# Low parts of a trunk's projection weights formed by accumulating DMA instead of VectorE

## The chip, the cores and the metric

One core of a Trainium2 chip runs the kernel. The metric is the device time of one execution in microseconds, the median of three runs. TensorE (PE) multiplies, VectorE (DVE), ScalarE (ACT) and GpSimd (POOL) do the element-wise work, SyncE (SP) issues most transfers, and 16 DMA engines move the bytes. A matmul here takes operands in a reduced 32-bit format (fp32r). Where full float32 accuracy is wanted, each operand is split into a high part (the value rounded to fp32r) and a low part (the value less its high part), and three matmuls are added up.

## The reference, cut to what matters

```
for layer in range(2):
    xn = rms_norm(h)                                   # (512, 1024)
    proj = xn @ w_in[layer]                            # w_in: 1024 x 4608, nine groups of 512 columns
    rq, rk, rv, rg, hq, hf_fwd, hf_bwd, hi, hg = split(proj)
    r_out = retention(rq, rk, rv) * silu(rg)           # 4 heads
    h_out = hgrn2(hq, hf_fwd, hf_bwd, hi) * silu(hg)   # 4 heads, both directions
    h = h + concat(r_out, h_out) @ w_out[layer]        # w_out: 1024 x 1024
    h = h + expert_choice_ffn(rms_norm(h))             # 16 SwiGLU experts, 64 tokens each
return rms_norm(h)
```

## The kernel before

A layer has two stages. The **mixer** makes the nine projections one after the other (proj 0 to proj 8; the order of the column groups is `GROUPS`), does the HGRN2 and retention work beside them, and ends with the output product with w_out. The **experts** stream their weights from HBM through the same slots.

Memory is cut into 22 slots of 8 KB per partition. `slot` takes the one that has been free longest, `put` gives one back; a new owner waits for the last readers of the old one. The weights w_in come as 18 tiles a layer of 1024 KB (512 rows by 512 columns, `raw`), two tiles per projection.

`split` makes the parts of half a tile (128 x 1024 elements) at a time: ScalarE copies it to the high part (line 436), and VectorE, in a few places GpSimd, subtracts to get the low part (line 438). `proj` is a generator: it goes through four quarters q of the contraction, 24 matmuls each (line 465), in threes: high weights with high input, low weights with high input, high weights with low input. So the second matmul of a quarter already needs the low part. At the start of quarter q, the split for quarter q + 1 is written. After every six matmuls it yields.

`lead` runs a projection and, at each yield, takes steps of a side generator until a budget is used up. That sets the order of the instructions on every engine; each engine then runs its own list strictly in that order and waits on semaphores. Beside proj 3 to proj 6 runs `hgrn`: per pair of heads a start (lines 568 to 583, whose results line 591 multiplies) and six levels, in which VectorE and GpSimd update factors (lines 551, 556, 561), ScalarE copies keys (line 531) and TensorE multiplies them (line 604). Beside proj 7 run the rest of it, the retention, and the first half of `wout_split`; beside proj 8 the norms and the second half. `wout_split` does for w_out what `split` does for w_in (lines 806 and 807). Evacuations of a projection's four PSUM banks (lines 477 and 478 for proj 1 and 2, line 503 for proj 7, lines 789 to 796 for proj 8) are ScalarE and VectorE work. `pump` loads tiles ahead, in the mixer at most two.

Of the kernel before, what the change touches and what calls it, by code (L numbers as in the profile page):

```python
# [10 lines left out]
F32R = mybir.dt.float32r  # L11
BF = mybir.dt.bfloat16
U8 = mybir.dt.uint8
AF = mybir.ActivationFunctionType
OP = mybir.AluOpType
# [50 lines left out]
class Kernel:  # L66
# [55 lines left out]
    def plan(self):  # L122
        a = self.a
        for l in range(self.depth):
            for g in self.GROUPS:
                for j in range(2):
                    n = 2 if g == self.GROUPS[0] and j == 0 else 1
                    self.wq.append((("in", l, g, j),
# [203 lines left out]
    def begin(self, l):  # L332

        self.mix_layer, self.nsplit, self.parts, self.wo = l, 0, {}, {}
        self.turned = {}

    def turn_in(self, ks, banks):
# [81 lines left out]
    COSTS = (1.2, 1.3, 0.65, 1.9)  # L419
    BUDGET = (1.0, 1.2, 1.0, 0.9, 2.2, 1.3)  # L420
    GROUPS = (4, 5, 6, 7, 0, 1, 2, 3, 8)

    def split(self, upto):


        nc = self.nc
        while self.nsplit <= min(upto, 4 * len(self.GROUPS) - 1):
            i = self.nsplit
            self.nsplit += 1
            g, j, jj = self.GROUPS[i // 4], i % 4 // 2, i % 2  # L430
            if jj == 0:
                self.raw = self.take(("in", self.mix_layer, g, j))
            part = self.slot([2, 2, 512], F32R)
            wh, low = part[:, 0], part[:, 1]
            src = self.raw.rearrange("p a k c -> p (a k) c")[:, 2 * jj:2 * jj + 2]
            nc.scalar.activation(wh, src, AF.Copy)  # L436
            e = nc.gpsimd if self.GROUPS[i // 4] in (7, 2) and i % 2 or i == 0 else nc.vector
            e.tensor_tensor(low, src, wh, op=OP.subtract)  # L438
            self.parts[i] = part
            if jj:  # L440
                self.put(self.raw)

    def proj(self, n, natural, evacuate):


        nc = self.nc
        pg = [self.pj() for _ in range(4)]
        for q in range(4):
            self.split(4 * n + q + 1)
            part = self.parts.pop(4 * n + q)  # L450
            wh, low = part[:, 0], part[:, 1]

            order = [(c, k2) for k2 in range(2) for c in range(4)] if n == 0 and q < 3 else \
                [(c, k2) for c in range(4) for k2 in range(2)]
            for i, (c, k2) in enumerate(order):
                cs = slice(c * P, (c + 1) * P)
                k = 2 * q + k2
                H, L = wh[:, k2], low[:, k2]
                xh, xl = self.xH[k // 4][:, k % 4], self.xL[k // 4][:, k % 4]
                if natural:  # L460
                    ops = ((xh[:, cs], H), (xh[:, cs], L), (xl[:, cs], H))
                else:
                    ops = ((H[:, cs], xh), (L[:, cs], xh), (H[:, cs], xl))
                for m, (lhsT, rhs) in enumerate(ops):
                    nc.tensor.matmul(pg[c], lhsT=lhsT, rhs=rhs, start=(k == 0 and m == 0), stop=(k == ND - 1 and m == 2))  # L465
                if k == ND - 1:
                    evacuate(c, pg[c])
                if i == 7:
                    self.put(part)
                if i % 2:  # L470
                    yield

# [325 lines left out]
    def wout_split(self, l):  # L798
        nc = self.nc
        for f in range(2):  # L800
            for j in range(2):
                raw = self.take(("out", l, f, j))
                wh, low = self.slot([4, 512], F32R), self.slot([4, 512], F32R)
                for i in range(2):
                    part = slice(2 * i, 2 * i + 2)
                    nc.scalar.activation(wh[:, part], raw[:, part], AF.Copy)
                    (nc.vector if i or f > j else nc.gpsimd).tensor_tensor(low[:, part], raw[:, part], wh[:, part], op=OP.subtract)  # L807
                    yield 0.6
                self.put(raw)
                self.wo[f, j] = (wh, low)  # L810

    def lead(self, gen, side=None, budget=0.0):


        credit = 0.0
        for _ in gen:
            self.pump(ahead=2, kinds=("in", "out"))
            credit += budget
            while side is not None and credit > 0.0:
                cost = next(side, None)  # L820
                if cost is None:
                    break
                credit -= cost

    def mixer(self, l):
        nc = self.nc
        self.norm1(l)
        self.rope = self.tmp4([2, S])
        nc.sync.dma_start(self.rope, self.a["rope"])
        if l == 0:  # L830
            self.const_rows()
        self.lead(self.proj(0, False, self.silu_q))
        if l == 0:
            self.more_consts()
        self.F = [self.slot([2, 2, S]) for _ in range(2)]
        self.K = [self.slot([2, 2, S]) for _ in range(2)]
        for n, d in ((1, 1), (2, 0)):
            self.lead(self.proj(n, False, lambda c, ps: self.forget(l, d, c, ps)))
        self.oh = None
        self.hsq = self.t2.tile([P, S], F32, name=f"hsq{l}", tag="tn", bufs=1)  # L840
        hg = self.hgrn()
        B = self.BUDGET
        self.lead(self.proj(3, True, lambda c, ps: self.copy_out("v2", c, ps)), hg, B[0])
        self.left = ()
        for n, nm in ((4, "rq"), (5, "rk")):
            self.lead(self.proj(n, False, lambda c, ps: self.rotate(nm, c, ps)), hg, B[n - 3])
        self.add_late()
        self.lead(self.proj(6, True, lambda c, ps: self.copy_out("rv", c, ps)), hg, B[3])
        wo = self.wout_split(l)

        def eighth():
            yield from hg
            yield from self.retention()
            for _ in range(4):
                yield next(wo)
        side = eighth()
        self.lead(self.proj(7, False, lambda c, ps: self.gate_out("rg", 4 * l, c, ps)), side, B[4])
        for _ in side:
            pass

        def ninth():
            yield from self.norms()
            yield from wo
        side = ninth()
        self.lead(self.proj(8, False, lambda c, ps: self.mix_out(8 + 4 * l, c, ps)), side, B[5])
        for _ in side:
            pass
        self.put(*self.xH, *self.xL, self.oh)
        self.load_h(self.hd if l > 0 else self.xv)
        self.xe = self.slot([ND, 2 * P])  # L870
        self.pump()
        self.output(l)
# [497 lines left out]
```

## Time and profile before

| | us |
|---|---|
| median of three runs | 1640.59 (1637.1 to 1641.18) |
| the profiled execution | 1637.67 |
| its span in the trace | 1635.8 |
| TensorE busy in the span | 1531.0 |
| VectorE busy | 664.4 |
| ScalarE busy | 474.9 |
| GpSimd busy | 229.3 |

The span is cut into stages in which different engines are the limit, so the shares of the whole say little about the mixer alone. Layer 0's mixer lies from 0 to 370 us (first expert matmul, line 1145), its experts from there to some 820 us, layer 1's mixer from there to 1179 us, and its experts take the rest. The profiled execution is 1.87 us longer than its span and 2.9 us shorter than the median.

### The profile page before, as it was taken

The numbers are of one execution on the slowest core, as the hardware profiler recorded it, in microseconds if no ns is written. First come the engines' busy times: TensorE is split into PE (matmuls) and PEld (weight loads), VectorE is DVE, ScalarE is ACT, GpSimd is POOL, SyncE is SP. The second block draws the span as 40 slices with busy tenths as digits, with TensorE's granted clock in tenths as the row PEclk, the third lists the DMA queues.
The fourth block names the chain that finished last, engine by engine and source line by source line (L and its number), as shares of the span: only waits on it lengthen the run. The fifth ranks groups of instructions, "written<-read, shape, count | busy, mean of one in ns | idle before, by whom it ended". The sixth has DMA issues, their size and how long they took to land. (4 is left out here: it accounts for less than half of the span.)

```text
span 1635.8 us, 19932 instructions
## 1 busy us (share of the span) xinstructions
PE 1531.0 (94%) x7970; PEld 954.9 (58%) x7970; DVE 664.4 (41%) x1107; ACT 474.9 (29%) x889; POOL 229.3 (14%) x201
## 2 busy tenths in 40 slices
PE   7989899969999999999999899999699999999986
PEld 6878798754354534533478787977444445444333
DVE  5378945561121312212254889464511122212113
ACT  4334444542221200200343434455322202112003
POOL 3042542100000000011021344430000000000201
PEclk9999999989999999999999999999799999999998
DMA  7211132577999999999941211317699999999997
GB/s 262 75 53 52 52 124 78 211 303 301 427 425 426 427 426 427 426 427 427 400 176 51 78 41 64 123 52 258 273 385 427 420 427 426 427 427 426 426 426 275
DMA packets 94605, 464.53 MB, mean 284 GB/s; under 512 B 7904, under 2 KB 16288, under 8 KB 48432
## 3 DMA queue, kind: packets, MB, share of 16 engines
q1 hardware_dynamic: 93040, 458.35, 69.0%
q0 software_dynamic: 1472, 4.90, 0.8%
q8 instruction: 63, 1.03, 0.2%
q14 instruction: 30, 0.25, 0.0%
HBM read 459.03 MB, written 4.19 MB: 283 GB/s over the span
## 5 line engine op out<-in xcount | busy, mean ns | idle before, releaser
L1145 PE MATMUL pj<-s,s 128*64 128x512 f32 x2048 | 478.8, 599 | 19.2 <-DMA s<-in_w_up_dram 13.9
L465 PE MATMUL pj<-s,s 128*128 128x512 f32 x1728 | 426.7, 401 | 12.9 <-DVE s L438 8.6
L465 PEld LDWEIGHTS pj<-s,s 128*128 128x128 f32 x1728 | 324.2, 192 | 82.7 <-DVE s L438 11.6
L1145 PEld LDWEIGHTS pj<-s,s 128*64 128x64 f32 x2048 | 173.3, 137 | 279.6 <-issue 203.3
L1265 PE MATMUL pb<-s,t 128*64 128x512 f32 x896 | 197.8, 594 | 5.4 <-ACT t L1183 2.7
L1272 POOL TENSOR_TENSOR s<-s,s 128x1024 f32<-128x1024 f32 x8 | 18.7, 2362 | 872.1 <-DVE s L1205 823.5
L1265 PEld LDWEIGHTS pb<-s,t 128*64 128x64 f32 x896 | 66.0, 137 | 126.8 <-issue 110.8
L1193 DVE SCALAR_TENSOR_TENSOR t<-pb,sm,t 128x512 fp32r<-128x512 f32 (+1 forms) x34 | 24.5, 719 | 242.5 <-ACT t L1192 241.0
L1205 DVE TENSOR_TENSOR s<-s,pb 128x512 f32<-128x512 f32 (+1 forms) x112 | 67.3, 661 | 130.0 <-PE pb L1200 130.0
L909 PE MATMUL pj<-s,s 128*128 128x512 f32 x384 | 96.6, 400 | 3.4 <-DVE s L796 2.9
L438 DVE TENSOR_TENSOR s<-s,s 128x1024 fp32r<-128x1024 f32 x62 | 84.3, 1383 | 37.8 <-ACT s L436 37.6
L1110 DVE COPY sm<-pb 128x2 f32<-128x2 f32 x16 | 2.5, 159 | 210.9 <-PE pb L1107 210.9
L909 PEld LDWEIGHTS pj<-s,s 128*128 128x128 f32 x384 | 69.3, 189 | 20.7 <-DVE s L796 4.6
L1192 ACT ACTIVATE t<-pb,sm 128x512 fp32r<-128x512 f32 (+1 forms) x34 | 22.5, 662 | 195.4 <-PE pb L1265 183.2
L1088 PEld LDWEIGHTS pb<-t,t 128*128 128x128 f32 x512 | 64.9, 199 | 17.3 <-issue 15.0
L1121 ACT ACTIVATE t<-pb 128x512 fp32r<-128x512 f32 x16 | 9.6, 601 | 221.0 <-PE pb L1119 221.0
L436 ACT ACTIVATE s<-s 128x1024 fp32r<-128x1024 f32 x72 | 73.4, 1048 | 0.0
L1088 PE MATMUL pb<-t,t 128*128 128x256 f32 x512 | 69.8, 293 | 3.2 <-DVE t L1072 2.4
L1200 PE MATMUL pb<-t,t 128*128 128x512 f32 (+1 forms) x256 | 66.7, 401 | 0.1
L556 DVE TENSOR_TENSOR s<-s,s 128x512 f32<-128x512 f32 x56 | 59.3, 1059 | 13.4 <-PE pb L604 13.4
L1200 PEld LDWEIGHTS pb<-t,t 128*128 128x128 f32 x256 | 44.7, 188 | 33.0 <-issue 19.4
L531 ACT ACTIVATE s<-s 128x256 f32<-128x256 f32 x96 | 35.3, 415 | 93.8 <-DVE s L551 93.5
(237 smaller groups left out, 1541.2 us busy)
## 6 DMA issues: line engine op xcount, KB each, us to landing
s<-in_w_gate_dram SPq DMA_DIRECT2D x124, 1024.0 KB, 19.5
s<-in_w_up_dram SPq DMA_DIRECT2D x124, 1024.0 KB, 19.6
s<-in_w_down_dram SPq DMA_DIRECT2D x112, 1024.0 KB, 19.6
s<-in_w_in_dram SPq DMA_DIRECT2D x34, 1024.0 KB, 5.9
s<-in_w_down_dram SPq DMA_DIRECT2D x32, 512.0 KB, 9.4
s<-in_w_out_dram SPq DMA_DIRECT2D x8, 1024.0 KB, 4.8
s<-in_x_dram SPq DMA_DIRECT2D x8, 512.0 KB
s<-in_w_gate_dram SPq DMA_DIRECT2D x8, 512.0 KB, 5.6
```

What stands on the lines that cost most here:

```text
L436: nc.scalar.activation(wh, src, AF.Copy)
L438: e.tensor_tensor(low, src, wh, op=OP.subtract)
L465: nc.tensor.matmul(pg[c], lhsT=lhsT, rhs=rhs, start=(k == 0 and m == 0), stop=(k == ND - 1 and m == 2))
L531: self.nc.scalar.activation(kv[:, :, e], src, AF.Copy)
L556: v.tensor_tensor(qv, qv, tq, op=OP.mult)
L909: nc.tensor.matmul(po, lhsT=x, rhs=w, start=(k == 0 and i == 0), stop=(k == ND - 1 and i == 2))
L1088: nc.tensor.matmul(pt[:, i], lhsT=x[:, tt, k % 2::2], rhs=oh[:, tt], start=(tt == 0 and x is self.picked[u][0]), stop=(tt == NT - 1 and x ...
L1145: nc.tensor.matmul(pg[n + 2 * f][e * CAP:(e + 1) * CAP], lhsT=self.xe[:, k, at + e * CAP:at + (e + 1) * CAP], rhs=w[e][:, f * 512:(f + 1) ...
L1193: v.scalar_tensor_tensor(yL[0][:, cs], py, gate, yH[0][:, cs], op0=OP.mult, op1=OP.subtract)
L1200: nc.tensor.matmul(pc, lhsT=ohT[:, tt * P:(tt + 1) * P], rhs=y[:, cs], start=(y is yH[0]), stop=(y is yL[0]))
L1205: v.tensor_tensor(dst, dst, pc, op=OP.add)
L1265: nc.tensor.matmul(py[f][e * CAP:(e + 1) * CAP], lhsT=hT[:, k, e * CAP:(e + 1) * CAP], rhs=W[e][:, k2, f * 512:(f + 1) * 512], start=(k == ...
```

## The change

For the first two projections of a layer nothing changes but the tiles: the parts of a whole raw tile now lie in two slots, one for the high and one for the low parts. From proj 2 on, and for w_out, ScalarE writes the high part and then its negative into the slot for the low part; a DMA issued from GpSimd's queue then adds the raw weights (128 x 2048 elements, 1024 KB) onto it in SBUF. The raw tile is given back after that DMA. The splits of a whole pair of quarters are written one pair ahead, at the start of every even quarter. The loads run one tile ahead in place of two.

```diff
+    N_ENGINE = 2
...
             if jj == 0:
                 self.raw = self.take(("in", self.mix_layer, g, j))
-            part = self.slot([2, 2, 512], F32R)
-            wh, low = part[:, 0], part[:, 1]
+                self.parts[i // 2] = self.slot([4, 512], F32R), self.slot([4, 512], F32R)
+            high, low = (x[:, 2 * jj:2 * jj + 2] for x in self.parts[i // 2])
             src = self.raw.rearrange("p a k c -> p (a k) c")[:, 2 * jj:2 * jj + 2]
-            nc.scalar.activation(wh, src, AF.Copy)
-            e = nc.gpsimd if self.GROUPS[i // 4] in (7, 2) and i % 2 or i == 0 else nc.vector
-            e.tensor_tensor(low, src, wh, op=OP.subtract)
+            nc.scalar.activation(high, src, AF.Copy)
+            if i < 4 * self.N_ENGINE:
+                (nc.gpsimd if i == 0 else nc.vector).tensor_tensor(low, src, high, op=OP.subtract)
+                if jj:
+                    self.put(self.raw)
+            else:
+                nc.scalar.activation(low, high, AF.Copy, scale=-1.0)
+                if jj:
+                    self.adds.append((self.parts[i // 2][1], self.raw))
...
+    def add_parts(self):
+        while self.adds:
+            low, raw = self.adds.popleft()
+            flat = "p a k c -> p (a k c)" if len(raw.shape) > 3 else "p k c -> p (k c)"
+            self.nc.gpsimd.dma_start(low.rearrange("p k c -> p (k c)"), raw.rearrange(flat), accum_op=OP.add)
+            self.put(raw)
...
         for q in range(4):
-            self.split(4 * n + q + 1)
+            self.split(4 * n + q + (1 if 4 * n + q + 1 < 4 * self.N_ENGINE else 3 - q % 2))
...
+                if i == 3:
+                    self.add_parts()
...
-                    nc.scalar.activation(wh[:, part], raw[:, part], AF.Copy)
-                    (nc.vector if i or f > j else nc.gpsimd).tensor_tensor(low[:, part], raw[:, part], wh[:, part], op=OP.subtract)
+                    nc.scalar.activation(high[:, part], raw[:, part], AF.Copy)
+                    nc.scalar.activation(low[:, part], high[:, part], AF.Copy, scale=-1.0)
                     yield 0.6
-                self.put(raw)
-                self.wo[f, j] = (wh, low)
+                self.adds.append((low, raw))
+                self.wo[f, j] = (high, low)
+                yield 0.0
+                self.add_parts()
...
-            self.pump(ahead=2, kinds=("in", "out"))
+            self.pump(ahead=1, kinds=("in", "out"))
...
-            for _ in range(4):
+            for _ in range(6):
                 yield next(wo)
```

ScalarE between proj 1 and proj 2 in layer 0, before: the last two evacuations of proj 1 (line 477 is its sigmoid, line 478 that of the negative), then the splits of the half tiles of proj 2.

```order
L477 ACTIVATE s_63_400<-pj_406 128x512
L478 ACTIVATE s_65_402<-pj_406 128x512
L436 ACTIVATE s_80_531<-s_54_324 128x1024
L436 ACTIVATE s_81_558<-s_72_443 128x1024
L436 ACTIVATE s_83_587<-s_72_443 128x1024
L436 ACTIVATE s_84_614<-s_75_501 128x1024
L477 ACTIVATE s_62_399<-pj_527 128x512
```

The same place now; lines 492 and 493 are the evacuations, 439 writes a high part, 445 its negative.

```order
L492 ACTIVATE s_63_399<-pj_405 128x512
L493 ACTIVATE s_65_401<-pj_405 128x512
L439 ACTIVATE s_80_533<-s_75_502 128x1024
L445 ACTIVATE s_81_534<-s_80_533 128x1024
L439 ACTIVATE s_80_533<-s_75_502 128x1024
L445 ACTIVATE s_81_534<-s_80_533 128x1024
L439 ACTIVATE s_83_590<-s_82_545 128x1024
L445 ACTIVATE s_84_591<-s_83_590 128x1024
```

The parts s_80 and s_81 are for the second half of proj 2, s_83 and s_84 for the first half of proj 3; each pair of quarters now has four activations in a row behind the evacuations, and an addition after them.

ScalarE at the end of proj 7 in layer 0, before: the last outputs of the retention (738, 740), four splits of w_out (806), the splits for the last quarter of proj 7 (s_246) and the first of proj 8 (s_247), and the evacuations of proj 7 (503).

```order
L738 ACTIVATE s_202_1668<-pb_1886 128x512
L740 ACTIVATE t_235_1839<-pb_1886 128x512
L806 ACTIVATE s_241_1901<-s_240_1899 128x1024 x2
L806 ACTIVATE s_244_1915<-s_243_1913 128x1024 x2
L436 ACTIVATE s_246_1927<-s_177_1451 128x1024
L436 ACTIVATE s_247_1954<-s_185_1551 128x1024
L503 ACTIVATE t_249_1964<-pj_1617 128x512
```

The same place now; 755 is the retention's last output, 821 and 822 write the parts of w_out, s_247 and s_248 are the parts for the first half of proj 8, 518 is the first evacuation.

```order
L755 ACTIVATE t_235_1852<-pb_1899 128x512
L821 ACTIVATE s_242_1916<-s_241_1914 128x1024
L822 ACTIVATE s_243_1917<-s_242_1916 128x1024
...
L821 ACTIVATE s_245_1931<-s_244_1929 128x1024
L822 ACTIVATE s_246_1932<-s_245_1931 128x1024
...
L439 ACTIVATE s_247_1943<-s_199_1645 128x1024
L445 ACTIVATE s_248_1944<-s_247_1943 128x1024
L439 ACTIVATE s_247_1943<-s_199_1645 128x1024
L445 ACTIVATE s_248_1944<-s_247_1943 128x1024
L518 ACTIVATE t_250_1982<-pj_1629 128x512
```

Twelve activations of 128 x 1024 elements now stand between the retention and the evacuations of proj 7, where six stood, and the parts for proj 8 are the last four of them.

GpSimd at the same place now: the last products of the retention (747), then four additions (454), of which the third (s_248) is for the first half of proj 8 and the first two are for w_out.

```order
L747 TENSOR_TENSOR s_234_1851<-s_126_1046,t_208_1692 128x384 x2
L454 DMA s_243_1917<-s_241_1914 128x2048
L454 DMA s_246_1932<-s_244_1929 128x2048
L454 DMA s_248_1944<-s_199_1645 128x2048
L454 DMA s_259_2017<-s_240_1912 128x2048
L791 TENSOR_TENSOR s_263_2032<-s_204_1685,s_261_2030 128x256
```

Before, GpSimd made two of the low parts of w_out here (line 807), and the low parts for proj 8 came from VectorE.

## Rows read from the trace of the kernel before

**Rows 1.** The page: one engine and the DMA tenths of 40 slices.

```profile
PE 1531.0 (94%) x7970; PEld 954.9 (58%) x7970; DVE 664.4 (41%) x1107; ACT 474.9 (29%) x889; POOL 229.3 (14%) x201
...
DMA  7211132577999999999941211317699999999997
```

**Rows 2.** Stretches: us, busy time of PE, PEld, DVE, ACT, POOL; granted clock; DMA.

```profile
60.00:80.00 20.00, 20.00 (x90) 16.57 (x89) 5.04 (x5) 6.92 (x10) 0.00 (x0) 1.00 0.06 16
...
93.00:105.00 12.00, 7.85 (x27) 5.59 (x26) 9.83 (x9) 4.65 (x8) 8.81 (x4) 0.72 0.26 87
...
164.00:172.00 8.00, 5.67 (x17) 3.88 (x16) 8.00 (x4) 2.31 (x4) 8.00 (x5) 0.79 0.15 39
...
192.00:200.00 8.00, 5.58 (x22) 4.40 (x21) 8.00 (x9) 2.39 (x5) 5.61 (x6) 0.79 0.00 0
...
410.00:820.00 410.00, 395.84 (x2008) 183.19 (x2008) 90.07 (x158) 70.34 (x139) 12.24 (x7) 1.00 1.01 424
...
900.00:910.00 10.00, 4.50 (x14) 2.60 (x13) 7.83 (x6) 3.06 (x3) 7.73 (x4) 0.79 0.31 106
```

**Rows 3.** Whom TensorE waited for, 0 to 400 us: total, times, longest.

```profile
PE pj L465 <- DVE s L438: 3.7, 2, 2.0
...
PE pb L591 <- POOL s L583: 4.5, 3, 2.2
...
PE pb L604 <- ACT s L531: 2.4, 1, 2.4
```

**Rows 4.** Instructions of lines 436 and 438: duration ns, smallest, median, largest.

```profile
L436 ACT ACTIVATE s<-s x72: 1039/1046/1062, 11.8 to 1098.4; 128x1024 fp32r<-128x1024 f32 x72
...
L438 DVE TENSOR_TENSOR s<-s,s x62: 1206/1224/3425, 19.5 to 1099.5; 128x1024 fp32r<-128x1024 f32 x62
...
L438 POOL TENSOR_TENSOR s<-s,s x10: 2342/2565/2887, 13.0 to 1017.1; 128x1024 fp32r<-128x1024 f32 x10
```

**Rows 5.** DMA issues: KB of each, median us from issue to landing.

```profile
s<-in_w_out_dram SPq DMA_DIRECT2D x8, 1024.0 KB, 4.8
...
hd<-s POOLq DMA_DIRECT2D x2, 1024.0 KB, 10.9
...
t<-in_dec_q_dram POOLq DMA_DIRECT2D x2, 512.0 KB, 3.9
...
t<-in_dec_in_dram POOLq DMA_DIRECT2D x2, 256.0 KB, 2.9
...
dec_k<-in_dec_k_dram POOLq DMA_DIRECT2D x1, 4.0 KB, 2.8
```

**Rows 6.** TensorE in order of time, layer 0: start us, us, what.

```profile
59.72 34.17 PE L465 MATMUL pj<-s,s 128*128 128x512 f32 x150
...
99.95 2.50 PE L465 MATMUL pj<-s,s 128*128 128x512 f32 x5 [1.96 <-DVE s L438]
...
256.75 8.68 PE L465 MATMUL pj<-s,s 128*128 128x512 f32 x37
...
267.17 6.87 PE L465 MATMUL pj<-s,s 128*128 128x512 f32 x29 [1.74 <-DVE s L438]
```

**Rows 7.** ScalarE in order of time, layer 0.

```profile
61.27 0.60 ACT L477 ACTIVATE s<-pj 128x512 f32<-128x512 f32 x1 [0.27 <-PE pj L465]
...
258.00 3.90 ACT L806 ACTIVATE s<-s 128x1024 fp32r<-128x1024 f32 x4
...
261.80 2.00 ACT L436 ACTIVATE s<-s 128x1024 fp32r<-128x1024 f32 x2
...
290.26 3.89 ACT L806 ACTIVATE s<-s 128x1024 fp32r<-128x1024 f32 x4
```

**Rows 8.** VectorE in order of time, layer 0.

```profile
260.05 5.93 DVE L807 TENSOR_TENSOR s<-s,s 128x1024 fp32r<-128x1024 f32 x2 [5.93 <-ACT s L806]
...
265.90 2.35 DVE L438 TENSOR_TENSOR s<-s,s 128x1024 fp32r<-128x1024 f32 x2
...
297.84 0.74 DVE L790 SCALAR_TENSOR_TENSOR t<-pj,cols,t 128x512 f32<-128x512 f32 x1
```

More of the change, by code (lines that the diff above doesn't have):

```diff
@@ L334, in begin @@
         self.mix_layer, self.nsplit, self.parts, self.wo = l, 0, {}, {}
+        self.adds = deque()
         self.turned = {}
@@ L432, in split @@
                 self.raw = self.take(("in", self.mix_layer, g, j))
-            part = self.slot([2, 2, 512], F32R)
-            wh, low = part[:, 0], part[:, 1]
+                self.parts[i // 2] = self.slot([4, 512], F32R), self.slot([4, 512], F32R)
+            high, low = (x[:, 2 * jj:2 * jj + 2] for x in self.parts[i // 2])
             src = self.raw.rearrange("p a k c -> p (a k) c")[:, 2 * jj:2 * jj + 2]
-            nc.scalar.activation(wh, src, AF.Copy)
-            e = nc.gpsimd if self.GROUPS[i // 4] in (7, 2) and i % 2 or i == 0 else nc.vector
-            e.tensor_tensor(low, src, wh, op=OP.subtract)
-            self.parts[i] = part
-            if jj:
-                self.put(self.raw)
+            nc.scalar.activation(high, src, AF.Copy)
[13 more added lines that the diff above has]
+            self.put(raw)
     def proj(self, n, natural, evacuate):
@@ L448, in proj @@
         for q in range(4):
-            self.split(4 * n + q + 1)
-            part = self.parts.pop(4 * n + q)
-            wh, low = part[:, 0], part[:, 1]
+            self.split(4 * n + q + (1 if 4 * n + q + 1 < 4 * self.N_ENGINE else 3 - q % 2))
+            high, low = self.parts[2 * n + q // 2]
             order = [(c, k2) for k2 in range(2) for c in range(4)] if n == 0 and q < 3 else \
@@ L457, in proj @@
                 k = 2 * q + k2
-                H, L = wh[:, k2], low[:, k2]
+                H, L = high[:, k % 4], low[:, k % 4]
                 xh, xl = self.xH[k // 4][:, k % 4], self.xL[k // 4][:, k % 4]
@@ L467, in proj @@
                     evacuate(c, pg[c])
-                if i == 7:
-                    self.put(part)
+                if i == 7 and q % 2:
+                    self.put(*self.parts.pop(2 * n + q // 2))
+                if i == 3:
+                    self.add_parts()
                 if i % 2:
@@ L802, in wout_split @@
                 raw = self.take(("out", l, f, j))
-                wh, low = self.slot([4, 512], F32R), self.slot([4, 512], F32R)
+                high, low = self.slot([4, 512], F32R), self.slot([4, 512], F32R)
                 for i in range(2):
                     part = slice(2 * i, 2 * i + 2)
-                    nc.scalar.activation(wh[:, part], raw[:, part], AF.Copy)
-                    (nc.vector if i or f > j else nc.gpsimd).tensor_tensor(low[:, part], raw[:, part], wh[:, part], op=OP.subtract)
+                    nc.scalar.activation(high[:, part], raw[:, part], AF.Copy)
+                    nc.scalar.activation(low[:, part], high[:, part], AF.Copy, scale=-1.0)
                     yield 0.6
-                self.put(raw)
-                self.wo[f, j] = (wh, low)
+                self.adds.append((low, raw))
+                self.wo[f, j] = (high, low)
+                yield 0.0
+                self.add_parts()
     def lead(self, gen, side=None, budget=0.0):
```

## The prediction

> **What bounds the kernel now.** I read the page first. TensorE is busy 94% of the span, and the tenths of the DMA engines show the two kinds of stage: 9 in the experts, 1 to 3 through most of the mixers [rows 1]. Then the windows. In the experts TensorE works 395.84 of 410 us and the DMA engines are full at 424 GB/s [rows 2]: both are limits there, the change touches neither, and the stretch begins when the mixer lets go of its slots. So a mixer that ends later moves the end of the program by about as much, and I count the mixers alone.
>
> In the mixers TensorE is full where nothing runs beside a projection (20.00 of 20 us from 60 to 80), and has gaps where HGRN2 does: 7.85 of 12 us from 93 to 105, at a granted clock of 0.72, and 8 us stretches with 5.67 and 5.58 us busy at 0.79 [rows 2]. A clock of 0.72 is a mean over time at 2.4 GHz and time at 1.2 GHz after a gap, so such a stretch loses its idle time plus busy time x (1 - clock): 4.15 + 2.2 = 6.4 us for the first, 2.33 + 1.2 = 3.5 and 2.42 + 1.2 = 3.6 for the others. VectorE is busy 8.00 of 8 us in the last two. The waits name the suppliers: 3.7 us for VectorE's line 438, which makes low parts, 4.5 for GpSimd's line 583, 2.4 for the keys of line 531 [rows 3]. That is the whole prize: some 13.5 us of HGRN2 stalls a layer, and 1.74 us at the end of proj 7 [rows 6].
>
> **What the change removes.** 48 subtractions on line 438 and 10 on line 807 leave VectorE, 8 and 6 leave GpSimd. At medians of 1.224 and 2.565 us [rows 4] this is 58 x 1.22 = 71 us and 14 x 2.57 = 36 us of engine time. VectorE's subtraction took up to 3.425 us: two of them took 5.93 us beside GpSimd at the end of proj 7 [rows 8]. None of it is path by itself; it counts only in the stalls above.
>
> **What it adds.** ScalarE gets 72 activations of 128 x 1024 at 1.046 us [rows 4], 75 us in all. It has room for the sum (6.92 busy of 20 us where TensorE is full, 2.4 to 4.7 in the stalls [rows 2]), so what matters is where they stand. And 36 additions of 1024 KB, 18 a layer. From a row of raw weights to a usable low part the way is now: four activations (about 4.2 us, or 3.9 when they follow closely [rows 7]), GpSimd's turn, and X, an addition from issue to landing.
>
> **The price of X.** No row shows an accumulating DMA. Below: a plain load of 1024 KB by SP lands after 4.8 us. Above: 1024 KB issued by GpSimd took 10.9 us, in two issues of one tile each [rows 5]. Between: GpSimd's transfers take 2.8 us for 4 KB, 2.9 for 256 KB and 3.9 for 512 KB [rows 5]; 2.7 us fixed and 1024 KB at 424 GB/s (2.5 us) would be 5.2. The addition also has to read the bytes it adds to, so I count its bytes twice: 2.7 + 2 x 2.45 = 7.6 us, and take that. The Trainium skill (DMA: Bandwidth & Descriptors, Rules for kernel authors) says that an accumulating DMA reads its destination and writes it later, which is the same step; no run here shows it yet. Its section on the GpSimd path there gives 2.0 us plus bytes over 436 GB/s, 4.4 us for this size by estimate; by that X would lie below my lower end, and the sum near 1620. The rows for small GpSimd transfers are 0.3 to 0.8 us slower than that formula, so I stay with the rows.
>
> **The places, one layer, layer 0's times.** A matmul of line 465 takes 34.17/150 = 0.228 us [rows 6], so half a projection is 48 x 0.228 = 10.9 us, a whole one 21.9.
>
> A. Second half of proj 2. Its four activations stand behind the evacuations of proj 1. The last pair of these starts at 61.27 [rows 7], when TensorE ends proj 1, and takes 1.2 us. 62.4 + 4.2 + 7.6 = 74.2; TensorE is there at 61.2 + 10.9 = 72.1. **+2.1**. (The first half is split one pair earlier and hidden by proj 1.)
>
> B. Second half of proj 3, where HGRN2 starts. Same arithmetic, another 2.1 us stall and 1.2 us of low clock, 3.3. But the 6.4 us of before go: line 438 is no longer in VectorE's or GpSimd's list there, and TensorE is late anyway. **-3.0**.
>
> C. The second pair of heads starts (164 to 172, 3.5 us lost). GpSimd's line 583 still has to come; half goes. **-1.8**.
>
> D. 192 to 200 (3.6 lost). Proj 5 alone takes four subtractions, 4.9 us, from a VectorE that was full; that is more than the 2.42 us gap. ScalarE's four activations in a row can hold up line 531, so I keep a third. **-2.5**.
>
> E. Start of proj 8. This one is dear. The retention's last output leaves ScalarE at 258.00 [rows 7]. Behind it now stand twelve activations (3 x 3.9 = 11.7 us) of which the last four are for proj 8, so its addition is issued at 269.7, behind two others of w_out whose bytes still move (1 us more), and lands at 278.3. TensorE has nothing else in its list: from 256.75 it makes the last 60 matmuls of proj 7 and would begin proj 8 at 270.4. Before it began at 267.17 + 24 x 0.228 = 272.6, with the 1.74 us stall in it [rows 6]. 278.3 - 272.6 = 5.7, and 2 us for the clock after a gap that long. **+7.7**.
>
> F. Proj 8's end. The last w_out tiles cost ScalarE eight activations where four took 3.89 us from 290.26 [rows 7]; the evacuations of proj 8 stand behind them. VectorE used to be the later one (line 790 only at 297.84 [rows 8]) and is now free, so of 4 us some 1.5 remain, and 0.5 for additions that meet the first expert loads. **+2.0**.
>
> The other eleven halves, the first of proj 2 among them: ScalarE and the addition need about 13 us, and from proj 4 on HGRN2's and the retention's own matmuls stretch a half to 15 us or more. Hidden; if X grows by 3 us, about 4 us a layer come out. GpSimd issues an addition only when the four activations are done, and what stands behind it in its list, HGRN2's factor updates (line 561, 576 now), waits up to 4 us with it; VectorE needs them one level later, some 7 us on, so I count nothing. The loads one ahead are hidden as well (5 us of load in a half of 11).
>
> **Sum.** 2.1 - 3.0 - 1.8 - 2.5 + 7.7 + 2.0 = 4.5 us a layer, 9 in all. On the profiled execution's own 1637.67 us this gives **1647 us**, 0.4% over the median of 1640.59, which is itself 2.9 us over that execution. A measurement of this kernel tells about 0.3% (4.9 us) from no change.
>
> With X at 4.8: A 0, B -5, C -3.5, D -3.6, E +3.1, F +1: -8 a layer, 1622 us. With X at 10.9: A +7.4, B +1, C 0, D -1, E +14 (the additions of w_out in front now queue), F +4, other halves +4: +29 a layer, 1697 us. Break-even is at X of about 6.6 us.
>
> **The rivals.**
> 1. The addition is cheap, X below 6.4 us, and the change is faster. For it: the DMA engines are at 1 to 3 tenths in the mixers, and plain loads land in 4.8. Against it: the second read and GpSimd's fixed 2.7. It gives 1622 to 1635. The skill's formula, named above, would put the kernel here. It decides at the start of proj 8: below 6.4 the stall there is worth less than what HGRN2 gets back. Chance 0.27.
> 2. The addition is dear, X of 10 or more: DMA engines add slower than they copy. For it: 10.9 for the h tile. Against: those two were issued together, so that one waits for the other's bytes. Every half of proj 4 to proj 7 then stalls as well: 1680 to 1697 or more. Chance 0.17.
> 3. ScalarE becomes what HGRN2 waits for. Four activations in a row stand in front of line 531's copies, which TensorE already waited 2.4 us for once [rows 3]. At each of five halves up to 3 us: +15 a layer, less C and D that do not come: about 1680. Against it: a level has two heads between, some 7 us of slack, and ScalarE was under half busy. Chance 0.08.
>
> **Chances.** My forecast, X between 6.4 and 10 and the places as above, holds 0.48; its own range is 1636 to 1668. Within it, X of 6.4 to 7.5 is within 0.3% of 1640.59 (0.2), the rest slower (0.28). So faster 0.27, same 0.2, slower 0.28 + 0.17 + 0.08 = 0.53. The range reaches into the first and second rival: 1624 to 1690.
>
> **What would show each step.** DMA issues: a row for line 454 with X. Waits: TensorE's line 478 waiting on a DMA, with the longest wait in each layer at the start of proj 8 (some 8 us), and about 2 us in the second halves of proj 2 and 3. Waits on GpSimd's line 598 (583 before) and on line 546 (531) shrink. VectorE's busy time falls by some 75 us, ScalarE's rises by as much. The windows of the experts stay as they are. I am wrong if the wait at proj 8 is under 3 us, if TensorE waits for line 546 more than before, or if the experts' stretch gets longer.

## The result, and the profile after

The changed kernel takes 1652.49 us in the median of four runs (1650.76 to 1653.2), the kernel before 1640.68 beside it: a ratio of 1.0075, 95% interval 1.0058 to 1.0093. It is slower by 11.8 us. The forecast of 1647 us was 6 over the median before and 9 over the profiled execution. The profiled execution took 1653.2 us with a span of 1651.0, so the spans differ by 15.2: before's profiled execution is one of its fastest, and this one the longest of its four. One execution in experiment 3 ran in a slower state (1952.1 us at a granted clock of 0.745) and is left out of the time given there.

**The page** of the kernel after: busy time and instructions of the engines, the DMA tenths of 40 slices, and the queue in which the additions run (packets, MB, share of 16 engines' span).

```profile
PE 1532.7 (93%) x7970; PEld 952.4 (58%) x7970; DVE 572.0 (35%) x1049; ACT 548.6 (33%) x961; POOL 218.0 (13%) x223
...
DMA  6554465877999999999944545469699999999997
...
q0 software_dynamic: 6656, 42.65, 12.0%
```

Against [rows 1], VectorE lost 92 us and ScalarE gained 74, and the DMA tenths of the mixers rose from 1 to 3 up to 4 to 7. TensorE's busy time is the same to 1.7 us. The work went where it was sent, so the loss is in waits and in the lower clock behind them.

**The stretches** of [rows 2] in the kernel after (the same columns; the stretches are fixed times, and work has shifted a little within them).

```profile
60.00:80.00 20.00, 18.62 (x83) 15.13 (x82) 0.00 (x0) 10.21 (x12) 1.72 (x2) 1.00 0.66 157
93.00:105.00 12.00, 9.70 (x38) 7.62 (x38) 11.71 (x11) 5.62 (x9) 8.07 (x5) 0.86 0.68 185
164.00:172.00 8.00, 6.49 (x32) 5.21 (x32) 8.00 (x8) 1.67 (x5) 6.51 (x4) 1.00 0.54 164
192.00:200.00 8.00, 7.23 (x39) 5.91 (x39) 6.48 (x11) 6.03 (x13) 1.78 (x5) 1.00 0.40 82
410.00:820.00 410.00, 396.72 (x1998) 181.17 (x1994) 88.54 (x147) 68.44 (x131) 9.36 (x4) 1.00 1.01 424
```

The three HGRN2 stretches are better than before, in busy time and in the granted clock (0.86, 1.00 and 1.00 for 0.72, 0.79 and 0.79). Proj 2, full before, has gaps. The experts are as they were.

**Whom TensorE waited for**, 0 to 400 us, after: total, times, longest.

```profile
PE pj L478 <- ACT s L445: 7.2, 1, 7.2
...
PE pb L606 <- POOL s L598: 3.5, 2, 2.0
...
PE pj L478 <- DMA s<-s: 2.4, 4, 1.4
...
PE pb L619 <- ACT s L546: 1.9, 2, 1.1
```

Compare [rows 3]: 3.7 us on line 438 are gone, GpSimd's factor (598, 583 before) went from 4.5 to 3.5, the keys (546, 531 before) from 2.4 to 1.9, and one wait of 7.2 us is new. In layer 1 the keys' wait is no shorter: 2.7 us, 2.4 before. TensorE in order of time shows where (start, us; in brackets the idle time before it; the row at 888.49 is layer 1's second half of proj 2):

```profile
73.91 8.41 PE L478 MATMUL pj<-s,s 128*128 128x512 f32 x36 [1.38 <-DMA s<-s]
...
97.22 1.42 PE L478 MATMUL pj<-s,s 128*128 128x512 f32 x5 [0.34 <-DMA s<-s]
101.06 1.22 PE L606 MATMUL pb<-s,parity 128*128 128x512 f32 x2 [1.96 <-POOL s L598]
...
268.80 0.50 PE L478 MATMUL pj<-s,s 128*128 128x512 f32 x1 [1.11 <-DVE s L519]
276.55 2.47 PE L478 MATMUL pj<-s,s 128*128 128x512 f32 x5 [7.25 <-ACT s L445]
278.95 1.94 PE L694 MATMUL pb<-t,pick 128*32 128x128 f32 x32
...
281.25 4.71 PE L478 MATMUL pj<-s,s 128*128 128x512 f32 x18
...
305.49 4.19 PE L926 MATMUL pj<-s,s 128*128 128x512 f32 x17 [0.72 <-DVE t L805]
...
888.49 23.43 PE L478 MATMUL pj<-s,s 128*128 128x512 f32 x95 [2.58 <-DMA s<-s]
```

The long wait is at the start of proj 8: the first matmul, which needs only a high part, runs at 268.80, and the second, which needs a low part, starts 7.25 us after its end. ScalarE and GpSimd at that place:

```profile
254.59 0.59 ACT L755 ACTIVATE t<-pb 128x512 f32<-128x512 f32 x1
255.07 1.06 ACT L821 ACTIVATE s<-s 128x1024 fp32r<-128x1024 f32 x1
...
266.42 1.06 ACT L445 ACTIVATE s<-s 128x1024 fp32r<-128x1024 f32 x1
...
275.40 1.06 ACT L445 ACTIVATE s<-s 128x1024 fp32r<-128x1024 f32 x1
```

```profile
259.56 0.89 POOL L454 DMA_DIRECT2D s<-s  x1 [7.39 <-ACT s L822]
...
268.01 0.85 POOL L454 DMA_DIRECT2D s<-s  x1 [3.23 <-issue]
```

The wait is labelled with ScalarE's line 445. That line ran again until 276.46, but those activations are for the second half of proj 8. The last one that the waiting matmul needs began at 266.42 and takes 1.06 us, so it had been done for 9 us. What came last is the addition issued at 268.01, 8.5 us before TensorE went on. The kernel of experiment 5, which copies in place of adding, confirms it: there TensorE went on at 270.58, before the later activations of line 445 had begun, and the label is the transfer.

```profile
270.58 2.08 PE L478 MATMUL pj<-s,s 128*128 128x512 f32 x5 [3.05 <-DMA s<-s]
...
271.59 1.06 ACT L445 ACTIVATE s<-s 128x1024 fp32r<-128x1024 f32 x1
```

A wait for two semaphores was put down to the wrong one here; which instruction of the named line is needed, and when it ended, tells it.

The mixers by their milestones: differences between the starts of the first matmul of each step on TensorE, in both profiled executions, layer 0 / layer 1. The first step counts from the span's start in layer 0 and from proj 0's first matmul in layer 1.

| from, to | before | after | change | forecast |
|---|---|---|---|---|
| start to HGRN2's first product (line 591, now 606) | 93.72 / 80.63 | 95.54 / 83.94 | +1.8 / +3.3 | +2.1 (A) |
| to the retention (721, 736) | 136.3 / 136.9 | 131.5 / 131.4 | -4.8 / -5.5 | -7.3 (B, C, D) |
| to the norms, six matmuls into proj 8 (679, 694) | 43.95 / 44.00 | 51.87 / 51.89 | +7.9 / +7.9 | +7.7 (E) |
| to the output product (909, 926) | 24.68 / 24.67 | 26.54 / 26.37 | +1.9 / +1.7 | +2.0 (F) |
| to the first expert matmul (1145, 1162) | 71.65 / 71.67 | 72.01 / 72.00 | +0.4 / +0.3 | 0 |
| mixer | 370.3 / 357.9 | 377.5 / 365.6 | +7.2 / +7.7 | +4.5 |
| experts to the next stage or the end | 451.3 / 456.4 | 450.3 / 457.6 | -1.0 / +1.2 | 0 |

A mixer that ends 7 us later does move the end by that much.

### The profile page after: what moved, and what is told of

It is laid out like the page before. It is cut to its first block, busy times and chain, and to the rows that moved or that the text cites. A ratio compares the mean times of both kernels' runs of the same rounds, so it can differ in the third digit from the quotient of the medians.

```text
span 1651.0 us, 19992 instructions
## 1 busy us (share of the span) xinstructions
PE 1532.7 (93%) x7970; PEld 952.4 (58%) x7970; DVE 572.0 (35%) x1049; ACT 548.6 (33%) x961; POOL 218.0 (13%) x223
## 4 chain that ended last, share of the span: by engine, by line
PE 51%; DMA 26%; issue 8%; DVE 7%; ACT 6%; POOL 2%; SPq 0%; DVEq 0%; POOLq 0%; ACTq 0%
DMA s<-in_w_up_dram 16%; PE pj L1162 16%; PE pj L478 10%; DMA s<-in_w_down_dram 7%; PE pb L1282 7%; PE pj L926 4%; PE pb L1105 3%; PE pb L619 2%; PE pb L1217 2%; DMA s<-s 2%; PE pb L1248 2%; PE pb L678 1%; POOL s L598 1%; ACT s L439 1%; PE pb L659 1%
## 5 line engine op out<-in xcount | busy, mean ns | idle before, releaser
L1105 PE MATMUL pb<-t,t 128*128 128x256 f32 x512 | 69.8, 293 | 3.2 <-DVE t L1089 2.4
L1183 ACT ACTIVATE t<-pj,sm 128x512 f32<-128x512 f32 x32 | 22.0, 687 | 140.8 <-PE pj L1162 125.7
L571 DVE TENSOR_TENSOR s<-s,s 128x512 f32<-128x512 f32 x56 | 51.0, 912 | 47.6 <-PE pb L619 47.6
L1217 PE MATMUL pb<-t,t 128*128 128x512 f32 (+1 forms) x256 | 66.6, 400 | 0.1
L454 POOL DMA_DIRECT2D s<-s x36 | 31.3, 870 | 220.2 <-ACT s L445 164.8
```

The source lines that it names most:

```text
L454: self.nc.gpsimd.dma_start(low.rearrange("p k c -> p (k c)"), raw.rearrange(flat), accum_op=OP.add)
L571: v.tensor_tensor(qv, qv, tq, op=OP.mult)
L1105: nc.tensor.matmul(pt[:, i], lhsT=x[:, tt, k % 2::2], rhs=oh[:, tt], start=(tt == 0 and x is self.picked[u][0]), stop=(tt == NT - 1 and x ...
L1217: nc.tensor.matmul(pc, lhsT=ohT[:, tt * P:(tt + 1) * P], rhs=y[:, cs], start=(y is yH[0]), stop=(y is yL[0]))
```

## The experiments

All are variants of the changed kernel, and ratios are to the kernel before. My theory: the loss stands at the start of proj 8 and is made by X, an addition from issue to landing, behind a row of ScalarE's activations. Rivals: X is no price of adding but of GpSimd's queue; ScalarE's row of four in front of HGRN2's keys eats the gain; loads one ahead are late.

**1. Proj 8 by the engines.**

```diff
-            if i < 4 * self.N_ENGINE:
+            if i < 4 * self.N_ENGINE or i >= 32:
```

> The low parts of proj 8 alone are made by VectorE's subtraction again; proj 2 to 7 and w_out keep the addition by DMA. Theory (the time is lost where proj 8 starts: TensorE waits 7.25 us a layer for an addition issued late, and runs at the low clock after it): the wait of 7.25 us is replaced by 1 to 2 us for ScalarE or VectorE, some 7 us a layer come back, and the kernel takes 1636 to 1640 us. Rival (the time is lost a little at every half tile, to ScalarE's and GpSimd's added load): two of fourteen halves a layer give back 1 to 2 us a layer, 1649 to 1651 us.

1637.11 us, 0.9982 (0.9973 to 0.9991). Retention to norms fell from 51.9 to 42.0 us in both layers, 10 us each, and norms to output rose from 26.5 to 28.2 and 29.1. Four subtractions a layer, which also spare ScalarE four activations and the DMA engines two additions, undo the whole loss, as the theory said.

**2. w_out by the engines**, proj 8 still by additions.

```diff
-                    nc.scalar.activation(low[:, part], high[:, part], AF.Copy, scale=-1.0)
+                    (nc.vector if i or f > j else nc.gpsimd).tensor_tensor(low[:, part], raw[:, part], high[:, part], op=OP.subtract)
...
-                self.adds.append((low, raw))
+                self.put(raw)
```

> w_out's low parts are made by VectorE and GpSimd again; all projections from proj 2 on keep the addition. Theory: the activations in front of those for proj 8 fall from eight to four, so its addition is issued 4.2 us earlier and without two others in front of it: the wait there falls from 7.25 us to about 3, with less time at the low clock after it; 5 to 6 us a layer, 1641 to 1644 us. Rival (spread load): 8 of 36 additions fewer, 1649 us. Second rival (the wait at proj 8 is for the loads or the slots, not for ScalarE's order): wait unchanged, 1652 us.

1642.83 us, 1.0025 (1.0016 to 1.0034): in the range, but not for my reason, since the wait only fell from 7.25 to 6.43 where I expected about 3. Retention to norms gave 2.2 us a layer, norms to output 1.0 and 1.3, output to experts 1.0 and 0.6. Proj 8's addition was issued at 263.37, 4.6 us earlier than in the changed kernel, and took 10.6 us to land. A load of w_out was issued 0.5 us ahead of it, at 262.88; in the changed kernel that load went out at 256.85. Two windows of this kernel:

```profile
264.00:268.00 4.00, 3.69 (x17) 2.72 (x15) 2.25 (x3) 1.36 (x4) 0.26 (x1) 1.00 0.92 249
268.00:272.00 4.00, 0.00 (x0) 0.00 (x0) 0.75 (x1) 3.88 (x5) 0.00 (x0) 1.00 1.11 236
```

The DMA engines (second to last column) are full while TensorE stands still. The trace's DMA records show in which order: the load's packets run from 263.91 to 268.74, the addition's first one starts at 267.99, 4.6 us after its issue, and its last one ends at 273.63. In the changed kernel an addition that finds the DMA engines free starts 1.45 us after its issue. So X is no constant: this addition started 3.2 us late, while the load's packets moved.

**3. No early step of w_out**: all its parts are made beside proj 8.

```diff
-            for _ in range(6):
+            for _ in range(0):
```

> All of w_out's splits are moved beside proj 8, none is left beside proj 7; the amount of work is the same as in the changed kernel. Theory: only the four activations for proj 8 stand behind the retention, its addition is issued 8 us earlier and lands before TensorE gets there: no wait at proj 8, 8 to 9 us a layer back. Against it, sixteen activations stand before the evacuations of proj 8, and the last additions land late: 1 to 5 us a layer. 1636 to 1645 us. Rival (spread load): no work has gone, so 1652 us.

1661.3 us, 1.0143 (1.0125 to 1.0162): my expectation failed. The wait at proj 8 did go (retention to norms 41.9 us), but norms to output grew to 34.9, and output to experts from 72.0 to 77.6 and 77.7, with a wait of 2.9 us for a late addition of w_out in it. ScalarE and then TensorE in this kernel:

```profile
284.60 1.05 ACT L821 ACTIVATE s<-s 128x1024 fp32r<-128x1024 f32 x1
...
297.91 1.06 ACT L822 ACTIVATE s<-s 128x1024 fp32r<-128x1024 f32 x1
...
300.28 0.60 ACT L804 ACTIVATE t<-pj 128x512 f32<-128x512 f32 x1
```

```profile
301.71 7.46 PE L926 MATMUL pj<-s,s 128*128 128x512 f32 x20 [5.73 <-DVE t L805]
```

Fourteen activations in a row stand in front of proj 8's evacuations (804, and VectorE's 805 behind it). TensorE waits 5.73 us, and its next 20 matmuls take 0.373 us each, where the changed kernel's first 17 took 0.246 (the row at 305.49 above). ScalarE's activations beside proj 8 are as little hidden as those ahead of it.

**4. The parts for proj 8 first**, then w_out's early steps.

```diff
                 yield from self.retention()
+            self.split(33)
             for _ in range(6):
```

> One line is added: the parts for the first half of proj 8 are written before the first w_out tiles instead of behind them. All work, every addition and the place of the later w_out splits are as in the changed kernel. Theory (the order of ScalarE's list makes the wait at proj 8): its addition is issued about 8 us earlier, alone, and lands 16 to 17 us after the retention's last output, while TensorE needs 14: a wait of 0 to 2 us in place of 7.25, 1637 to 1641 us. Rival (the additions as such cost the time, wherever they stand): 1650 to 1653 us.

1645.04 us, 1.0036 (1.0023 to 1.005): better than the change, but 4 us over my range. Retention to norms 43.3 us, so the stall at proj 8 is gone; norms to output 31.9 and 31.6, where TensorE waits 3.7 us for the norms' line 707 on ScalarE. The four activations for the second half of proj 8 stand in front of the norms there; in the changed kernel they ran while TensorE stood still. So part of the stall comes back one step later on the same engine. Whether an order with the norms in front of them would avoid that was not tried.

**5. A copy in place of the addition.** This leaves the sum out: the low part is overwritten with the raw weights.

```diff
-            self.nc.gpsimd.dma_start(low.rearrange("p k c -> p (k c)"), raw.rearrange(flat), accum_op=OP.add)
+            self.nc.gpsimd.dma_start(low.rearrange("p k c -> p (k c)"), raw.rearrange(flat))
```

> The 36 transfers copy the raw weights in place of adding them: the computation is changed (low parts hold the whole weights), order and sizes are not. Theory (an addition moves its bytes twice, since it reads what it adds to): issue to landing falls from 7.8 us to about 5.3, the wait at proj 8 from 7.25 to some 5 us, those at the second halves of proj 2 and 3 vanish: 3 to 4 us a layer, 1644 to 1647 us. Rival (the time from issue to landing is fixed work of GpSimd's path, not bytes): 7 to 8 us still, 1652 us.

1633.35 us, 0.9968 (0.9956 to 0.9981): faster than either expectation; the copy lands after 4.3 us, where I expected 5.3. The row of the issues, and the queue's share, for the copy:

```profile
q0 software_dynamic: 6656, 42.65, 6.8%
...
s<-s POOLq DMA_DIRECT2D x36, 1024.0 KB, 4.3
```

and line 454 (the additions) in the changed kernel, with its landing times:

```profile
L454 POOL DMA_DIRECT2D s<-s x36: 847/871/911, 48.4 to 1119.2; - x36
...
DMA to landing us min/median/max: 6.8/7.8/11.7
```

The queue of the kernel before, which has no such transfers:

```profile
q0 software_dynamic: 1472, 4.90, 0.8%
```

Same queue, same bytes, same place: the copy lands after 4.3 us and the queue holds the DMA engines for 6.8% of the span, the addition 7.8 us and 12.0%. Without the 0.8% of other transfers it is 6.0 and 11.2%, 1.9 times. The wait at proj 8 falls to 3.0 us. Adding costs 3.5 us; the queue is not the price. The program gains 19.1 us from it, 5.5 for each us of X (17.5 and 5.0 by the ratios). Some of this may be GpSimd's, which is busy 0.59 us with issuing a copy and 0.87 with an addition; that was not tried apart.

**6. Twice the negative** for proj 3 to proj 6, 16 more activations a layer, which change no value.

```diff
-                nc.scalar.activation(low, high, AF.Copy, scale=-1.0)
+                for _ in range(2 if 12 <= i < 28 else 1):
+                    nc.scalar.activation(low, high, AF.Copy, scale=-1.0)
```

> In proj 3 to 6 the negative is written twice by ScalarE: 32 activations of 128 x 1024 more in all, 33 us of ScalarE, each addition there issued 2.1 us later; nothing else changes. Theory (ScalarE's added work beside HGRN2 lies in slack; additions have 0 to 5 us to spare there): 1 to 4 us a layer, 1654 to 1660 us. Rival (four activations in a row are what HGRN2's keys wait for): two more in each batch cost 2 us at most of the eight halves, 1665 us or more.

1667.3 us, 1.017 (1.0154 to 1.0186): 14.8 us over the changed kernel for 32 activations, so the rival holds. From HGRN2's first product to the retention it takes 8.6 and 7.7 us longer, 0.5 us for each of them. TensorE's waits from 85 to 230 us in this kernel (lines one higher than in the changed one), and in the changed one:

```profile
PE pb L607 <- POOL s L599: 6.6, 4, 2.4
PE pb L620 <- ACT s L547: 4.9, 3, 2.9
```

```profile
PE pb L606 <- POOL s L598: 3.5, 2, 2.0
PE pb L619 <- ACT s L546: 1.9, 2, 1.1
PE pj L478 <- DMA s<-s: 1.1, 3, 0.5
```

From 93 to 230 us ScalarE is busy for 83.0 of 137 us (74.2 in the changed kernel, 57.3 before). The wait for the keys (547), which stand behind the longer rows, grew by 3.0 us, and the one for GpSimd's factors (599) by 3.1. The second is a path that I had put at nothing: GpSimd stands at an addition until ScalarE's row is done, and its factors come after it (the second pair of heads, layer 0):

```profile
164.06 0.87 POOL L455 DMA_DIRECT2D s<-s  x1 [5.18 <-ACT s L446]
```

**7. The negative by VectorE** for proj 3 to proj 6: does the row at its present length cost?

```diff
-                nc.scalar.activation(low, high, AF.Copy, scale=-1.0)
+                if 12 <= i < 28:
+                    nc.vector.tensor_scalar(low, high, -1.0, None, op0=OP.mult)
+                else:
+                    nc.scalar.activation(low, high, AF.Copy, scale=-1.0)
```

> The changed kernel, but for proj 3 to proj 6 VectorE and not ScalarE writes the negative of the high part (32 operations, 16 a layer). Theory: what the HGRN2 stretch lost to the change is ScalarE's row of four activations in front of the keys' copies; 32 more of them cost 14.8 us, 0.46 us each, so taking 32 away should give back 8 to 14 us, less what VectorE's new work costs: 1639 to 1646 us, and the time from HGRN2's first product to the retention falls below 128 us in layer 0 (131.4 in the changed kernel). Rival: the extra activations hurt only because the row grew longer than the slack, and at its present length it is hidden; then nothing is gained and VectorE's work costs: 1651 to 1658 us.

1654.32 us, 1.009 (1.0074 to 1.0105): no gain, so the rival holds again. HGRN2's start to the retention got longer, 133.7 us for 131.5 and 134.0 for 131.4, where kernels that are alike in this stretch differ by up to 1.7 us. TensorE's waits from 85 to 230 us:

```profile
PE pb L609 <- POOL s L601: 5.0, 4, 2.4
PE pb L622 <- ACT s L549: 2.0, 1, 2.0
```

The wait for the keys is again 2 us in all. In the changed kernel it was two, 0.77 us behind ScalarE's row and 1.12 for VectorE's line 566; here the first is gone, and the second has grown to 1.98. The wait for the factors grew from 3.5 to 5.0. So the row at its present length does cost a little, and VectorE's sixteen operations a layer of 0.694 us take back at least as much.

**8. Loads two ahead**, as before the change.

```diff
-            self.pump(ahead=1, kinds=("in", "out"))
+            self.pump(ahead=2, kinds=("in", "out"))
```

> The changed kernel with raw tiles loaded two ahead, as before the change, in place of one. My step was that the loads one ahead are hidden: 1650 to 1654 us. Rival: the one tile ahead makes splits late somewhere in the mixers, and the time falls by 3 us or more, below 1649.5; a slot held longer could also cost, above 1655.

1649.21 us, 1.0052 (1.0039 to 1.0064). That is 3.3 us under the changed kernel, but the two were measured apart and their intervals overlap: at the edge of what can be told. The plainest place is the end of proj 8. In the changed kernel ScalarE waits 0.93 us for a load of w_out in front of proj 8's evacuations, and TensorE 0.72 us for these; with loads two ahead both waits are gone in both layers, and norms to output is 0.9 and 1.3 us shorter.

```profile
298.49 1.06 ACT L821 ACTIVATE s<-s 128x1024 fp32r<-128x1024 f32 x1 [0.93 <-DMA s<-in_w_out_dram]
```

Proj 2 of layer 1, where the wait for an addition fell from 2.58 to 1.43 us, is no such place: with loads one ahead the kernels of experiments 3 and 7 have 1.42 and 1.39 there.

**9 to 12. Versions that avoid the dear places.** Proj 8 and w_out by engines (edits 1 and 2 together); then proj 2 and proj 8 (`N_ENGINE = 3` and edit 1); then all three, so that additions remain for proj 3 to proj 7; then this with loads two ahead.

> w_out and proj 8 are split by VectorE and GpSimd again, proj 2 to 7 keep the addition. Theory: beyond proj8_engine (1637 us) this takes 16 activations a layer-pair half from ScalarE near the evacuations of proj 8, where TensorE waited 1.46 us for line 805 and 1.6 us for line 717; but VectorE's and GpSimd's subtractions stand there again as before: 1633 to 1638 us. Rival (w_out's additions are free once proj 8 does not wait for them): same as proj8_engine within 2 us. Rival (w_out's subtractions slow the end of proj 7): 1640 us or more.

> Proj 2 and proj 8 are split by VectorE again, proj 3 to 7 and w_out keep the addition. Theory: the waits for an addition at the second half of proj 2 go (1.4 us with a little low clock, 1.8 and 3.3 us a layer by the shift of the first HGRN2 matmul): 3 to 5 us below proj8_engine, 1632 to 1635 us. Rival (TensorE is only early there and waits for HGRN2's start instead): same as proj8_engine, 1637 us.

> The additions only where something covers them: proj 0 to 2, proj 8 and w_out by the engines, proj 3 to 7 by additions. If what the two kernels with proj 2 and 8, and with proj 8 and w_out, by engines gained adds up (proj 2's part is the difference of 1637.1 and 1630.2, some 7 us; w_out's that of 1637.1 and 1630.6, some 6.5 us), it is 1623 to 1626 us. If both gains are the same few us seen from two sides, it is 1629 to 1631.

> The kernel with additions for proj 3 to proj 7 alone (1626.0 us), with raw tiles loaded two ahead in place of one. The changed kernel with two ahead came out 3.3 us shorter, at the edge of what can be told. If loads one ahead do make splits late, and not only where the changed kernel stalls for its additions, this gives 1621 to 1624 us; if the loads are hidden, or what two ahead gave lay at proj 2 and proj 8, 1625 to 1628.

| additions for | us | ratio, 95% interval |
|---|---|---|
| proj 2 to 7 | 1630.61 | 0.9946 (0.9933 to 0.9958) |
| proj 3 to 7 and w_out | 1630.21 | 0.9939 (0.9926 to 0.9952) |
| proj 3 to 7 | 1626.03 | 0.9918 (0.9904 to 0.9931) |
| proj 3 to 7, loads two ahead | 1622.88 | 0.9903 (0.9886 to 0.9919) |

The first two came out 2 us better than expected, the third at the upper end of the first range (11.1 of the 13.4 us add up), the last in the first of its ranges. Its four runs (1622.01 to 1623.89) lie below all four of the third (1624.79 to 1627.77), so loads one ahead seem to cost some 3 us here too, though the ratios' intervals overlap. Again w_out shows it: with loads one ahead ScalarE waits 3.0 and 3.2 us for its last tile (layer 0 below), with two ahead not at all, and output to experts falls from 70.8 and 71.1 to 69.7 and 69.8 us.

```profile
285.06 2.01 ACT L821 ACTIVATE s<-s 128x1024 fp32r<-128x1024 f32 x2 [2.96 <-DMA s<-in_w_out_dram]
```

This kernel beats both. In it retention to norms takes 41.9 us and norms to output 26.1, where the kernel before has 44.0 and 24.7. How much of the gain comes from the additions, and how much from splits that are now written a pair ahead, was not tried apart.

## Why the prediction was right, and where it was not

The direction, the mechanism of the main term (E) and its place were right; the size was 3 to 6 us short. Of the smaller terms D failed, and B and F came near for other reasons than forecast. By its steps:

- **X**, taken as 7.6 (bounds 4.8 and 10.9), is 7.8 in the median. The step "I count its bytes twice" is what the runs show: 3.5 us more than the copy, with 1.9 times the DMA engines' time for the same bytes. The Trainium skill (DMA: Bandwidth & Descriptors, Rules for kernel authors) says that an accumulating DMA reads its destination and writes it later; the doubled time agrees with a second read, while the order of the two no run shows. The Trainium skill's formula for the GpSimd path (same page, Anatomy of one DMA — SWDGE (gpsimd) path), 4.4 us by estimate, fits the copy (4.3) and not the addition.
- **A** was right in layer 0: the addition was issued at 66.92 (forecast 66.6), TensorE came to it at 72.5 (72.1) and went on at 73.91 (74.2). In layer 1 the wait is 2.58 us, and 1.6 us of low clock follow: 95 matmuls take 23.43 us, 21.80 in layer 0. The splits were not late there; the addition was issued at 880.32, right behind its activations, and took 8.0 us to land. Of the 16 DMA engines 15 had reported at 887.19 and the last one at 888.36. Why that one lagged is open. "The loads one ahead are hidden as well" did fail, but at the end of proj 8 (experiment 8).
- **B, C, D** were over-valued together, -4.8 and -5.5 for -7.3. The parts come from the starts of the HGRN2 products in layer 0 (line 604, 619 now).
- **B**: at the end of the first pair of heads the lead over before is 0.7 us (139.80 to 139.11), which with A's 1.8 makes B -2.5 (forecast -3.0). That is near by luck, as both its terms were too large. The forecast stall of 2.1 us and 1.2 of low clock was a wait of 0.34 us (at 97.22). In its place GpSimd's line 598 still made TensorE wait 1.96 us (at 101.06), and by the window from 93 to 105 us 2.3 + 9.70 x 0.14 = 3.7 of the 6.4 us were still lost.
- **C**: at the second pair's first product the lead is 3.3 (171.93 to 168.59), C -2.6 (-1.8).
- **D**: at the last product the lead is 4.1 (215.8 to 211.7), so D gave 0.8 of its 2.5. The gap there was the wait of 2.4 us for the keys [rows 3]; 1.12 and 0.77 us of it are left. At the first of the two, ScalarE's copy itself waited for VectorE's line 566, which is not a subtraction (rows below). At the second, the copies began at 195.09, right behind the four activations for the parts. So taking the subtractions from VectorE did not close the gap. The retention starts 2.9 us earlier, so 1.2 more went, 0.93 of it in a wait for line 665 that was not there before. This line's delay was not traced further.

```profile
190.38 0.72 ACT L546 ACTIVATE s<-s 128x256 f32<-128x256 f32 x2 [3.12 <-DVE s L566]
191.20 1.13 PE L619 MATMUL pb<-s,s 128*128 128x128 f32 x8 [1.12 <-ACT s L546]
```

- **E** was right in size, +7.9 for +7.7: twelve activations from 255.07 to 267.48 (12.4 us for 11.7), the addition issued at 268.01 and usable 8.5 us later (8.6). All of it lies 1 to 2 us earlier than forecast, on both sides. The +7.9 are the wait of 7.25, 1.11 for proj 7's evacuations behind the twelve activations (at 268.80, not in the sum) and 1.3 of low clock (five matmuls in 2.47 us), less the 1.74 of before. The low clock's other 1.4 us fall behind the norms' start, so it cost 2.7 for 2.0.
- **F** was right in size, +1.9 and +1.7 for +2.0, but by luck. In layer 0 1.4 us of it are this low clock, from the norms' first matmul to line 717: compare the rows at 278.95 and 281.25 with the same ones before, below. The place that F priced, proj 8's evacuations, gave 0.46 (line 805, 0.72 us for 0.26), and that came from the load of w_out (experiment 8).

```profile
273.96 1.08 PE L679 MATMUL pb<-t,pick 128*32 128x128 f32 x32
...
275.19 4.38 PE L465 MATMUL pj<-s,s 128*128 128x512 f32 x18
```

- **Rivals.** The first fell on X (experiment 5), but its pricing held: a transfer of 4.3 us makes the same program faster. With 5.5 us of program for each us of X, break-even is near 7.8 - 11.8/5.5 = 5.7 us by estimate (forecast 6.6; my slope on this side, 25 us for X from 7.6 to 4.8, was 9). A larger X was not tried. The second did not come. The third was half right: at the rows' present length moving the negatives to VectorE gains nothing (7), but "ScalarE was under half busy" was no argument, as another 16 activations a layer cost 8 us (6). There GpSimd, standing at an addition, delayed its factors, for which I had counted nothing.
- **"The other eleven halves: hidden"** held in layer 0 but for 1.0 us, in layer 1 but for 1.9.
- **VectorE's busy time**, a sign and no term, fell by 92 us and not by 75. Part of this is that what stayed got shorter: line 556 (571 now), 56 operations, went from 59.3 to 51.0 us.

By the spans the two mixers lost 14.9 us where 9 were forecast. The 6 us between are B to D (2.5 and 1.8 less gained), A in layer 1 (1.2) and the output product (0.4 and 0.3). The medians ask for 11.8 and not 15.2; these few us are variation between runs that no experiment here resolves.

## What to carry to other kernels

Work moved to a transfer must be priced as a latency at each place where its result is first needed, and kept only where something covers it: here proj 3 to proj 7, beside HGRN2 and the retention, and not proj 2, proj 8 or w_out. An engine that is half busy may have no slack where it supplies a chain; a doubled instruction there shows it in one run. When a wait names a line, find the instruction of it that is needed and when that ended: 9 us earlier means that something else came last.

## What the runs showed of the hardware

**An adding transfer uses the DMA engines about twice.** The changed kernel while TensorE waits for proj 8 (columns as in [rows 2]):

```profile
268.00:272.00 4.00, 0.50 (x1) 0.19 (x1) 2.25 (x3) 1.40 (x3) 0.85 (x1) 0.96 1.01 207
272.00:276.00 4.00, 0.00 (x0) 0.00 (x0) 0.75 (x1) 3.94 (x5) 0.00 (x0) 0.50 0.95 197
```

The engines are full at some 200 GB/s of counted bytes, and at 424 GB/s in the experts. In the trace's DMA records an addition that meets nothing moves its 1024 KB in 5.1 us, the copy of experiment 5 in 2.7.

**A transfer waits for what the DMA engines already move.** The three additions at the end of proj 7 were issued at 259.56, 263.94 and 268.01 and moved their bytes from 261.07 to 266.14, 266.00 to 271.18 and 271.01 to 276.08, one behind the other. The slowest of the 36 (11.7 us) was issued at 230.19, 2.6 us behind a load, and started 4.7 us after its issue.

**The clock after the stall.** In these two windows the granted clock goes from 0.96 to 0.50, the 1.2 GHz level, while TensorE idles, and its first five matmuls then take 0.494 us each, against 0.228 at 2.4 GHz.
